# Dilated projections ahead of the gates among the filler products, and the last unit of the first mixer's output held back

## The chip, the cores and the metric

One core of a Trainium2 chip runs the whole program. The metric is the time of one execution in device microseconds (us), taken as the median of several runs. TensorE (PE) multiplies, ScalarE (ACT) and VectorE (DVE) read its results from PSUM, GpSimd (POOL) does small side work, SyncE (SP) issues the loads.

## What is computed

Two transformer blocks in sequence on 256 tokens of width 1024, in float32. The first has differential and stick-breaking attention, a cross attention and an MLP. The second, where the change lies, is cut here to what matters:

```python
proj = h @ w_in                       # queries, keys, values, gates of both mixers
q_a, k_c, v_c, k_s, v_s, k_w, v_w, g_nsa, q_b, k_b, v_b, g_ma, g_mb = split(proj)
y_a = nsa(rope(norm(q_a)), k_c, v_c, rope(norm(k_s)), v_s, rope(norm(k_w)), v_w, sigmoid(g_nsa))
y_b = dilated(rope(norm(q_b)), rope(norm(k_b)), v_b)      # 3 dilations, 4 heads each
m = sigmoid(g_ma) * (y_a @ w_o_a) + sigmoid(g_mb) * (y_b @ w_o_b)
x = x + m @ w_out                     # and the second block's MLP behind it
```

The first mixer (`nsa`) has 12 query heads in 3 key groups and adds three attentions: over keys compressed from blocks, over selected keys (`kts`) and over a window (`ktw`).

## The kernel before, in words

**Products.** Every float32 product is made of three fast ones: each operand is split into a high and a low part (`act` is `acth` and `actl`, a weight is `whi` and `wlo`), and PE runs high x high, low x high and high x low (L266 to L268 with the result transposed, L319 to L321 otherwise, L334 and L335 in the accumulation behind the mixers). A weight unit is 1024 x 256: SP loads it in two halves of 512 KB into `wraw` (6 buffers, L223), ACT copies the high part (L232), DVE subtracts for the low part (L233), 8 buffers each. One unit takes 48 such products (3 x 8 x 2), a unit of `w_o_a` 36.

**Order.** The program is written as attention steps with products put between them. A `Filler` holds a list of generators; `fill(n)` runs products from the first generator on until an amount `n` of work is done, and `flush()` runs all that is left. Out of this program a scheduler with its own estimates of durations makes the final order of each engine, and each engine then takes its instructions strictly in that order. Tiles share buffers by size class (`CLASSES`, L148): the biggest class, `c8` of 2048 floats a partition, has 8 buffers, used by the split activations, by the gates (`gm`), by the compression weights (`cw`) and by others.

**The second block.** `block2` projects the queries of the first group and all keys and values (`kv`, L1084). `nsa_keys` normalizes and rotates the keys: squares on ACT (L1151), their sums and an inverse root in small steps on DVE and ACT (L375 to L380), the scaling (L1156) and rotation (L1166, L1170) on DVE with POOL multiplying beside it (L1164); the result is `kn`, one tile for each 128 tokens. Its transposes on PE (L427) are evicted by ACT into `kts` and `ktw` (L619). The first `Filler` holds the query units 1 and 2 and the two compressions (L1036, with 1 MB loads of `cw`, L1032). Query evictions are L1178 (L1182 after the change, where `norm_rope_k`'s L1156, L1164, L1166, L1170 are L1160, L1168, L1170, L1174). The second `Filler` holds gate A (`gate_project`, 4 units), the dilated projections (`dil_project`, 9 units) and gate B, and, appended later, `first_mixer_out` (L1359), 4 units of the first mixer's output. They lie between the score and value steps of the first mixer and then of the two dilated head pairs (`dil_scores`, `dil_values`: transposes of probabilities L427, values L637 and L640, normalizer L1340). A pair's output is `dy` (L1428), split into `y`.

**The end of the mixers.** After the flush, the second mixer's output is accumulated over its two chunks of 128 (L266 to L268 into PSUM), weighted and added to the first mixer's (`evac_b`), split (L286 on ACT), and multiplied by `w_out` (L334). Matters for this end:

```python
acc = self.acc_new(True)
w = self.wrows(I["w_o_b_2"], 0)
for mp in range(4):
    for j in range(2):
        self.acc_add(acc, w, j, yc(6 + j), j == 0, j == 1, (2 * mp, 2 * mp + 1))
    evac_b(mp, acc[mp])
```

Of the kernel before, what the change touches and what calls it, by code (L numbers as in the profile page):

```python
# [10 lines left out]
F32R = mybir.dt.float32r  # L11
I32 = mybir.dt.int32
AF = mybir.ActivationFunctionType
# [4 lines left out]
P = 128  # L18
T = 256
NT = 2  # L20
D = 1024
KC = 8
HD = 64
# [102 lines left out]
def run(gen):  # L126
    for _ in gen:
        pass
# [6 lines left out]
class Builder:  # L135
# [381 lines left out]

    def sb_heads(self, q, k, v, ys, F):

# [3 lines left out]
        for c in range(2):  # L523
# [8 lines left out]
            for a in range(2):  # L532
                nc.scalar.activation(e[:, 2 * c + a], zs[2 * c + a][:, :384], AF.Abs)
        F.fill(3)
        x = nc.scalar.activation(e, e, AF.Exp, scale=-1.0)
        self.with_tables("natural_log", x, [lambda: nc.scalar.activation(e, e, AF.Ln, bias=self.one)])
        F.fill(3)
        ps, made = [], []
        for i, z in enumerate(zs):
            s = self.t([P, 384], "p", self.NP)  # L540
            nc.vector.scalar_tensor_tensor(out=s, in0=z[:, :384], scalar=0.0, in1=e[:, i], op0=ALU.max, op1=ALU.add)
            for c0 in (0, 256):
                self.strict(s[:, c0:c0 + P])
            F.fill(0.7)
            mm(z[:, 0:256], self.tri, s[:, 0:256], start=False, stop=True, skip_group_check=True)
# [7 lines left out]
            made.append(i)  # L553
        F.fill(1.5)
        for c in range(2):
# [3 lines left out]
            self.split1(ys[c][0], ys[c][1], po)  # L559
            F.fill(1)  # L560

# [524 lines left out]
    def nsa_keys(self, kv):  # L1086

        nc = self.nc
        gate = self.t([P, 3, NSA_H, 2], "gate")
        e = self.t([P, NT, 36], "gatee")  # L1090
        nc.scalar.activation(e, kv[:, :, 768:804], AF.Exp, scale=-1.0)
        nc.vector.tensor_scalar(out=e, in0=e, scalar1=1.0, scalar2=None, op0=ALU.add)
        for tt in range(NT):
            nc.vector.reciprocal(out=gate[:, :, :, 1 - tt], in_=e[:, tt].rearrange("p (h b) -> p b h", b=3))
        kn = [self.t([P, 6, 2, HD], "kn") for _ in range(NT)]
        xs = [kv[:, tt, 0:768].rearrange("p (a b) -> p a b", b=384)[:, :, 0:192].rearrange("p a (h d) -> p a h d", d=HD)
              for tt in range(NT)]
        self.norm_rope_k(xs, kn)
        kts = self.t([P, 3, 256], "kts")
        ktw = self.t([P, 3, 256], "ktw")  # L1100

        def transposed():
            for g in range(3):
                for dst, h in ((kts, g), (ktw, 3 + g)):
                    self.k_pair_t(dst[:, g, 0:256], [kn[tt][:, h] for tt in range(NT)])
            return kts, ktw, gate
        return transposed

    def cmp_keys(self, hk, hv):


        nc, mm = self.nc, self.nc.tensor.matmul
        o = self.Oo()
        for m in range(2):
            mm(o[0:48, 0:HD], hk[:, m], self.w2k[:, m], start=(m == 0), stop=(m == 1))
        kc = self.t([48, 1, HD], "kcn")
        nc.scalar.activation(kc[:, 0], o[0:48, 0:HD], AF.Copy)
        kcn = self.t([48, 1, 2, HD], "kcd")
        self.norm_rope([kc], lambda tt, i: self.rtc[:, i], [kcn[:, :, 0]], 1)
        nc.vector.tensor_copy(kcn[:, :, 1], kcn[:, :, 0])  # L1120
        ps = self.X()
        self.transpose(ps[:, 0:48], kcn.rearrange("p a b d -> p (a b d)"))
        kct = self.t([P, NSA_G, 2, 16], "kct")
        nc.gpsimd.memset(kct, 0.0)
        for a in range(2):
            rs = slice(64 * a, 64 * a + 64)
            nc.scalar.activation(kct[rs, :, a], ps[rs, 0:48].rearrange("p (g c) -> p g c", c=16), AF.Copy)
        rep = self.t([P, 2, 3, 4, 16], "hvrep")
        for m in range(2):
            nc.vector.tensor_copy(rep[:, m], hv[:, m].rearrange("p (g c) -> p g c", c=16)[:, :, None, :].to_broadcast(  # L1130
                [P, 3, 4, 16]))
        o = self.Oo()
        for g in range(3):
            for m in range(2):
                mm(o[0:64, g * HD:(g + 1) * HD], rep[:, m, g].rearrange("p r c -> p (r c)"), self.w2v[:, m],
                   start=(m == 0), stop=(m == 1))
        vx = self.t([P, 3, 4, HD], "vx")
        nc.gpsimd.memset(vx[64:128], 0.0)
        ov = o[0:64, 0:192].rearrange("p (g d) -> p g d", d=HD)
        for h in range(4):  # L1140
            nc.scalar.activation(vx[0:64, :, h], ov, AF.Copy, scale=self.headsel[:, h:h + 1])
        return kct, vx

    def norm_rope_k(self, xs, kn):

# [100 lines left out]
    def nsa_values(self, g, c, ps_, f, kv, vx, pct, y, F, work):  # L1246
        po = self.Oo((P, T))
        for b in range(2):
            for a in range(2):
                self.scale_rows(ps_[a, b], f[:, b, a])  # L1250
            pts = [self.probs_t(ps_[a, b]) for a in range(2)]
            if b == 0:
                self.nc.tensor.matmul(po, vx[:, g, 2 * c:2 * c + 2].rearrange("p a d -> p (a d)"), pct, start=True,
                                      stop=False, skip_group_check=True)
            F.fill(2 * work)
            vs = slice(192 + 384 * b + HD * g, 192 + 384 * b + HD * g + HD)
            self.pv2(po, [kv[:, 0, vs]] * 2, [kv[:, 1, vs]] * 2, pts, False, b == 1)
        self.split1(*y, po)
# [97 lines left out]
            nc.scalar.activation(s, s, AF.Ln, bias=self.one)  # L1356
            nc.scalar.activation(s, s, AF.Exp, scale=-1.0)

    def first_mixer_out(self, y, gates):  # L1359

        nc = self.nc
        for u in range(4):
            o = []
            w = self.wunit(self.I["w_o_a_2"][:, 256 * u:256 * u + 256].rearrange("(k p) n -> p k n", p=P), 6, 256)
            yield from self.gemm_t([w], y, o, nk=6)
            g = gates[0][:, 2 * u:2 * u + 2]
            nc.vector.tensor_tensor(out=g, in0=g, in1=o[0], op=ALU.mult)

    def block2(self, h):
        nc, I = self.nc, self.I  # L1370
        hc = lambda k: h[:, k]
        act = self.act(hc, self.gg)
        ss, ss2 = self.sumsq(h, self.g["g_final"])
        rf, rrn = self.rstd_n([ss, ss2], D, "rrn")
        rb = self.row(rrn, "rb")
# [7 lines left out]
        F = Filler(self.nsa_queries(act, rrn, 1, qs[1]), self.compress(bs[0], I["cmp_k_w1_2"], hk),  # L1383
                   self.nsa_queries(act, rrn, 2, qs[2]), self.compress(bs[1], I["cmp_v_w1_2"], hv))
        F.fill(FILL_KEYS)
        kts, ktw, gate = keys()
        F.fill(FILL_KEYS)
        self.nsa_queries_t(*qs[0])
        F.fill(1)
        y = (self.t([P, KC, T], "acth", dt=F32R), self.t([P, KC, T], "actl", dt=F32R))  # L1390
        yc = lambda k: (y[0][:, k], y[1][:, k])
        dil, gates = {}, []
        sc, pct = {}, {}
        sc[0, 0] = self.nsa_scores(0, 0, qs[0][0], kts, ktw, gate, F, FILL_SCORES)
        sc[0, 1] = self.nsa_scores(0, 1, qs[0][0], kts, ktw, gate, F, FILL_SCORES)
        F.flush()
        F = Filler(self.gate_project(act, rb, 4260, gates), self.dil_project(act, rrn, dil),
                   self.gate_project(act, rb, 5284, gates))
        kct, vx = self.cmp_keys(hk[0], hv[0])
        F.fill(2)  # L1400
        pc = self.nsa_cmp(0, qs[0][0], kct, gate)
        for g in range(NSA_G):
# [3 lines left out]
            pct = self.nsa_cmp_t(pc)  # L1406
            for c in range(2):
# [5 lines left out]
                elif c == 0:  # L1413
                    while 0 not in dil:
                        F.fill(1.0)
                    sc[0] = self.dil_scores(*dil[0][:2], F, FILL_DIL_SCORES)
        F.gens.append(self.first_mixer_out(y, gates))
        for pair in range(2):
            po = self.Oo((P, 2, T))
            values = self.dil_values(po, *sc.pop(pair), dil[pair][2], F, FILL_DIL_VALUES)  # L1420
# [10 lines left out]

        mx = (self.t([P, KC, T], "acth", dt=F32R), self.t([P, KC, T], "actl", dt=F32R))

        pins = []

        def evac_b(mp, o):
            sl = slice(2 * mp, 2 * mp + 2)
            g = gates[1][:, sl]
            a = nc.vector.tensor_tensor(out=g, in0=g, in1=o, op=ALU.mult)
            b = nc.vector.tensor_tensor(out=g, in0=g, in1=gates[0][:, sl], op=ALU.add)  # L1440
            pins.append((a, b, self.split1(mx[0][:, sl], mx[1][:, sl], g)))
        acc = self.acc_new(True)
        w = self.wrows(I["w_o_b_2"], 0)
        for mp in range(4):
            for j in range(2):
                self.acc_add(acc, w, j, yc(6 + j), j == 0, j == 1, (2 * mp, 2 * mp + 1))
            evac_b(mp, acc[mp])
        order = [pins[i][j] for i, j in ((0, 0), (0, 1), (1, 0), (1, 1), (0, 2), (2, 0), (2, 1), (1, 2),
                                             (3, 0), (3, 1), (2, 2), (3, 2))]
        for x, y in zip(order, order[1:]):  # L1450
# [3 lines left out]
        for k in range(KC):  # L1454
            i = nc.vector.scalar_tensor_tensor(out=h[:, k], in0=h[:, k], scalar=self.g["g_final"][:, k:k + 1],
                                               in1=rf, op0=ALU.mult, op1=ALU.mult)
# [62 lines left out]
```

## Time and profile before

| what | value |
|---|---|
| median of 3 runs | 881.71 us (881.45 to 884.4) |
| the profiled execution | 880.0 us, span 877.8 us |
| busy PE | 860.9 us (98%) |
| busy DVE, ACT, POOL | 602.1, 551.9, 95.6 us |
| granted clock of PE | 1.00 throughout |
| share of the last chain: PE, ACT, DMA, DVE | 92%, 3%, 2%, 2% |

Busy times are of one profiled execution, on the only core. PE is the engine that sets the time; the other engines' idle time costs nothing by itself. A matmul's own duration is drawn until its modelled end, so neighbours overlap: what counts is the distance between starts.

### The profile page before, as it was taken

To read this page: it belongs to the slowest core of one execution; us is meant where nothing else is said; L and a number is where in the kernel's file an instruction comes from. 1 tells how busy PE (TensorE), PEld (TensorE's weight loads), DVE (VectorE), ACT (ScalarE), POOL (GpSimd) and SP (SyncE) were. 2 spreads that over 40 slices of the span, in tenths; PEclk is the share of its full clock that TensorE was granted. 3 is DMA by queue.
4 is the path that set the end of the run, shared out by engine and by line. 5 is a ranking of instruction groups with operands and counts; after the bars stand their busy time and mean duration, and the time that the engine had idled before them with its cause. 6 is when DMAs were issued, how large, how long until landed. Compare 5 with 4: busy or idle time off the path is not lost.

```text
span 877.8 us, 18311 instructions
## 1 busy us (share of the span) xinstructions
PE 860.9 (98%) x7109; PEld 828.0 (94%) x7109; DVE 602.1 (69%) x1291; ACT 551.9 (63%) x1199; POOL 95.6 (11%) x139
## 2 busy tenths in 40 slices
PE   7999999999999999999999999999988999999998
PEld 6989999999999999999998999889978999999997
DVE  7645687585597555675877786686947975555554
ACT  5769577464575555664674887877764665555551
POOL 4032100020020000000203130113410300000000
PEclk9999999999999999999999999999999999999999
DMA  9655445653466766766387354232623565666541
GB/s 312 182 183 155 143 133 157 193 171 94 144 177 181 217 192 184 229 200 205 83 256 245 121 164 125 73 86 84 213 101 96 165 211 181 189 192 187 183 136 49
DMA packets 111830, 144.68 MB, mean 165 GB/s; under 512 B 6272, under 2 KB 100096, under 8 KB 111744
## 3 DMA queue, kind: packets, MB, share of 16 engines
q1 hardware_dynamic: 111600, 143.50, 53.2%
q8 instruction: 55, 0.90, 0.4%
q14 instruction: 31, 0.25, 0.1%
q10 hardware_dynamic: 144, 0.03, 0.0%
HBM read 142.46 MB, written 1.05 MB: 163 GB/s over the span
## 4 chain that ended last, share of the span: by engine, by line
PE 92%; ACT 3%; DMA 2%; DVE 2%; issue 1%; POOL 0%; SPq 0%; ACTq 0%; DVEq 0%; POOLq 0%
PE G L266 12%; PE G L267 12%; PE G L268 12%; PE G L320 5%; PE G L321 5%; PE G L319 5%; PE Z L268 4%; PE Z L267 4%; PE Z L266 4%; PE X L266 4%; PE X L268 4%; PE X L267 4%; PE X L427 3%; DMA wraw<-w_in 2%; PE Z L627 2%; PE O L640 1%
## 5 line engine op out<-in xcount | busy, mean ns | idle before, releaser
L233 DVE TENSOR_TENSOR wlo<-wraw,whi 128x512 fp32r<-128x512 f32 (+1 forms) x512 | 348.8, 696 | 167.4 <-ACT whi L232 164.6
L232 ACT ACTIVATE whi<-wraw 128x512 fp32r<-128x512 f32 (+1 forms) x512 | 313.6, 624 | 201.6 <-PE G L268 83.6
L267 PE MATMUL G<-acth,wlo 128*128 128x256 f32 x892 | 251.2, 283 | 4.3 <-DVE wlo L233 4.3
L266 PE MATMUL G<-acth,whi 128*128 128x256 f32 x892 | 252.3, 284 | 0.6 <-DVE gm L1352 0.3
L268 PE MATMUL G<-actl,whi 128*128 128x256 f32 x892 | 249.0, 283 | 0.0
L267 PEld LDWEIGHTS G<-acth,wlo 128*128 128x128 f32 x892 | 168.4, 189 | 6.0 <-DVE wlo L233 5.1
L266 PEld LDWEIGHTS G<-acth,whi 128*128 128x128 f32 x892 | 168.8, 189 | 2.6 <-issue 0.8
L268 PEld LDWEIGHTS G<-actl,whi 128*128 128x128 f32 x892 | 167.0, 189 | 0.3
L319 PE MATMUL G<-whi,acth 128*128 128x256 f32 x400 | 114.0, 286 | 0.0
L320 PE MATMUL G<-wlo,acth 128*128 128x256 f32 x400 | 114.0, 285 | 0.0
L321 PE MATMUL G<-whi,actl 128*128 128x256 f32 x400 | 114.0, 285 | 0.0
L320 PEld LDWEIGHTS G<-wlo,acth 128*128 128x128 f32 x400 | 75.5, 189 | 1.4 <-issue 0.8
L319 PEld LDWEIGHTS G<-whi,acth 128*128 128x128 f32 x400 | 75.4, 189 | 1.4 <-ACT whi L232 0.4
L321 PEld LDWEIGHTS G<-whi,actl 128*128 128x128 f32 x400 | 75.5, 189 | 1.0 <-issue 0.8
L266 PE MATMUL X<-mhl,whi 128*128 128x256 f32 x240 | 67.6, 282 | 0.5 <-DVE mt L1471 0.5
L268 PE MATMUL Z<-mhl,whi 128*128 128x256 f32 x240 | 67.5, 281 | 0.0
L268 PE MATMUL X<-mhl,whi 128*128 128x256 f32 x240 | 67.4, 281 | 0.0
L266 PE MATMUL Z<-mhl,whi 128*128 128x256 f32 x240 | 67.3, 281 | 0.0
L267 PE MATMUL X<-mhl,wlo 128*128 128x256 f32 x240 | 67.3, 280 | 0.0
L267 PE MATMUL Z<-mhl,wlo 128*128 128x256 f32 x240 | 67.3, 280 | 0.0
L266 PEld LDWEIGHTS X<-mhl,whi 128*128 128x128 f32 x240 | 45.3, 189 | 0.7 <-DVE mt L1471 0.7
L654 ACT ACTIVATE p<-p,mx 128x256 f32<-128x256 f32 x88 | 39.0, 446 | 10.2 <-DVE mx L647 6.1
(393 smaller groups left out, 1523.0 us busy)
## 6 DMA issues: line engine op xcount, KB each, us to landing
wraw<-w_up SPq DMA_DIRECT2D x64, 512.0 KB, 3.9
wraw<-w_down SPq DMA_DIRECT2D x64, 512.0 KB, 3.6
wraw<-w_in SPq DMA_DIRECT2D x42, 512.0 KB, 4.6
wraw<-w_dil SPq DMA_DIRECT2D x18, 512.0 KB, 4.1
wraw<-w_xkv SPq DMA_DIRECT2D x16, 512.0 KB, 3.7
wraw<-w_out SPq DMA_DIRECT2D x16, 512.0 KB, 3.7
wraw<-w_in SPq DMA_DIRECT2D x22, 256.0 KB, 5.5
wraw<-w_xq SPq DMA_DIRECT2D x8, 512.0 KB, 3.8
```

The source lines that it names most:

```text
L232: nc.scalar.activation(hi, r, AF.Copy)
L233: i = nc.vector.tensor_tensor(out=lo, in0=r, in1=hi, op=ALU.subtract)
L266: mm(out, w[0], x[0], start=first, stop=False, skip_group_check=True)
L267: mm(out, w[1], x[0], start=False, stop=False, skip_group_check=True)
L268: mm(out, w[0], x[1], start=False, stop=last, skip_group_check=True)
L319: mm(outs[tt], x[0][:, k, ts_], w[0], start=first, stop=False, skip_group_check=True)
L320: mm(outs[tt], x[0][:, k, ts_], w[1], start=False, stop=False, skip_group_check=True)
L321: mm(outs[tt], x[1][:, k, ts_], w[0], start=False, stop=(k == KC - 1), skip_group_check=True)
L427: self.mark = self.nc.tensor.transpose(out, in_, self.ident[:n, :n])
L627: i = mm(z[:, 0:256], q[rs, P:T], k[rs, 0:256], start=True, stop=True)
L640: mm(po[rs], v0[a], pts[a][:, 0:256], start=False, stop=last, skip_group_check=True)
L654: self.nc.scalar.activation(s[:, sl], s[:, sl], AF.Exp, scale=-1.0, bias=m[:, i:i + 1], accum_out=sums[:, i:i + 1])
```

## The change

Three edits. The dilated projections come first in the second `Filler`, then gate A and gate B. The transposed keys `kts`, `ktw` and the compressed values of groups 0 and 1 share one tile of the biggest class (`kt2`), the values of group 2 get a small one, and the tile pair `y` is taken only after the first flush. And `first_mixer_out` gets a list of units: 0 to 2 stay among the fillers, while unit 3 runs at the end, in the middle of the second mixer's accumulation, whose first chunk is now added for all outputs ahead of the second.

```diff
-        kts = self.t([P, 3, 256], "kts")
-        ktw = self.t([P, 3, 256], "ktw")
+        self.kt2 = self.t([P, 2048], "kt2")
+        kts, ktw = [self.kt2[:, 768 * i:768 * i + 768].rearrange("p (g k) -> p g k", k=256) for i in range(2)]
...
-        vx = self.t([P, 3, 4, HD], "vx")
-        nc.gpsimd.memset(vx[64:128], 0.0)
+        v01 = self.kt2[:, 1536:2048].rearrange("p (g h d) -> p g h d", g=2, d=HD)
+        v2 = self.t([P, 4, HD], "vx")
...
-    def first_mixer_out(self, y, gates):
+    def first_mixer_out(self, y, gates, us):
...
-        for u in range(4):
+        for u in us:
...
-        y = (self.t([P, KC, T], "acth", dt=F32R), self.t([P, KC, T], "actl", dt=F32R))
-        yc = lambda k: (y[0][:, k], y[1][:, k])
...
         F.flush()
-        F = Filler(self.gate_project(act, rb, 4260, gates), self.dil_project(act, rrn, dil),
+        y = (self.t([P, KC, T], "acth", dt=F32R), self.t([P, KC, T], "actl", dt=F32R))
+        yc = lambda k: (y[0][:, k], y[1][:, k])
+        F = Filler(self.dil_project(act, rrn, dil), self.gate_project(act, rb, 4260, gates),
                    self.gate_project(act, rb, 5284, gates))
...
-        F.gens.append(self.first_mixer_out(y, gates))
+        F.gens.append(self.first_mixer_out(y, gates, range(3)))
...
+        self.acc_add(acc, w, 0, yc(6), True, False)
         for mp in range(4):
-            for j in range(2):
-                self.acc_add(acc, w, j, yc(6 + j), j == 0, j == 1, (2 * mp, 2 * mp + 1))
+            self.acc_add(acc, w, 1, yc(7), False, True, (2 * mp, 2 * mp + 1))
             evac_b(mp, acc[mp])
+            if mp == 1:
+                run(self.first_mixer_out(y_a, gates, (3,)))
```

The scheduler makes a new order out of it. **PE, behind the second query unit.** `G_1088` (before) and `G_1087` (after) are that unit's result, `X` are banks for transposes, `kn` the keys, `Z` scores, `cw` compression weights; a "waits" names the engine whose result is awaited. Before:

```order
L321 MATMUL G_1088_6166<-whi_1086_6162,actl_970_5571 128x256
L1036 MATMUL G_1103_6268<-cw_1104_6269,bk_1017_5850 48x256 [waits DMAHW3_49]
L1036 MATMUL G_1103_6268<-cw_1104_6269,bk_1017_5850 48x256 x7
L1036 MATMUL G_1103_6268<-cw_1107_6287,bk_1017_5850 48x256 [waits DMAHW4_49]
L1036 MATMUL G_1103_6268<-cw_1107_6287,bk_1017_5850 48x256 x7
L319 MATMUL G_1139_6376<-whi_1131_6360,acth_969_5570 128x256 [waits Activation_49]
...
L319 MATMUL G_1139_6376<-whi_1137_6372,acth_969_5570 128x256
L427 MATMUL X_1089_6209<-c_ident_110,kn_1066_6107 128x128 [waits DVE_49]
L427 MATMUL X_1090_6213<-c_ident_110,kn_1066_6107 128x128
L320 MATMUL G_1139_6376<-wlo_1138_6373,acth_969_5570 128x256
```

After:

```order
L321 MATMUL G_1087_6165<-whi_1085_6161,actl_970_5571 128x256
L427 MATMUL X_1088_6208<-c_ident_110,kn_1066_6107 128x128 [waits DVE_49,Activation_49]
L427 MATMUL X_1089_6212<-c_ident_110,kn_1066_6107 128x128 [waits Activation_49]
L427 MATMUL X_1088_6208<-c_ident_110,kn_1067_6108 128x128 [waits DVE_49]
L427 MATMUL X_1089_6212<-c_ident_110,kn_1067_6108 128x128
L427 MATMUL X_1090_6216<-c_ident_110,kn_1066_6107 128x128 [waits Activation_49]
...
L427 MATMUL X_1105_6281<-c_ident_110,qn_1007_5771 128x128 [waits Activation_49]
L427 MATMUL X_1105_6281<-c_ident_110,qn_1007_5771 128x128
L627 MATMUL Z_1108_6290<-kt2_1075_6143,qt_1016_5849 128x256 [waits Activation_49]
...
L1036 MATMUL G_1102_6267<-cw_1103_6268,bk_1017_5850 48x256 [waits DMAHW4_49]
```

The key and query transposes and the first scores moved ahead of the compression product and of the whole third query unit (43 of its 48 products stood ahead of the first transposes before).

**ACT, around the keys' inverse root** (`rsy`; `qn` are the evicted queries of the second unit). Before:

```order
L232 ACTIVATE whi_1137_6372<-wraw_1130_6358 128x512 [waits DVE_49]
L376 ACTIVATE rsy_1072_6116<-rsv_1071_6115 128x12 [waits DVE_49]
L377 ACTIVATE rsy_1072_6116<-rsy_1072_6116 128x12 [waits Activation_49]
L232 ACTIVATE whi_1188_6590<-wraw_1186_6586 128x512 [waits DMAHW0_49,PE_49]
L232 ACTIVATE whi_1190_6594<-wraw_1186_6586 128x512 [waits PE_49]
L1178 ACTIVATE qn_1077_6145<-G_1088_6166,rrn_985_5640 128x256 [waits PE_49,Pool_49]
```

After:

```order
L232 ACTIVATE whi_1191_6602<-wraw_1186_6592 128x512 [waits DMAHW5_49,DVE_49,PE_49]
L376 ACTIVATE rsy_1072_6116<-rsv_1071_6115 128x12 [waits DVE_49]
L1182 ACTIVATE qn_1076_6144<-G_1087_6165,rrn_985_5640 128x256 [waits PE_49,Pool_49]
L377 ACTIVATE rsy_1072_6116<-rsy_1072_6116 128x12 [waits Activation_49]
L1182 ACTIVATE qn_1076_6144<-G_1087_6165,rrn_985_5640 128x256
```

The second step of the root now stands behind an eviction that waits for PE's second query unit.

**PE, at the end of the mixers.** `O_1672`, `G_1671` and their like are banks of the second mixer's accumulation, `Z_1687` and `Z_1686` the first of `w_out`. Before:

```order
L1340 MATMUL O_1615_8658<-diag_1617_8660,ones_68 64x256
L266 MATMUL O_1672_8970<-acth_1108_6290,whi_1677_8979 128x256 [waits DVE_49]
...
L268 MATMUL O_1672_8970<-actl_1109_6291,whi_1681_8987 128x256
L334 MATMUL Z_1687_9071<-acth_1667_8965,whi_1693_9079 128x256 [waits Activation_49]
```

After:

```order
L1344 MATMUL O_1592_8538<-diag_1594_8540,ones_68 64x256
L266 MATMUL O_1662_8920<-acth_1168_6534,whi_1667_8929 128x256 [waits DVE_49]
...
L268 MATMUL O_1662_8920<-actl_1169_6535,whi_1671_8937 128x256
L266 MATMUL G_1681_9001<-acth_1168_6534,whi_1675_8989 128x256 [waits DVE_49]
...
L268 MATMUL G_1681_9001<-actl_1169_6535,whi_1679_8997 128x256
L334 MATMUL Z_1686_9075<-acth_1657_8915,whi_1692_9083 128x256 [waits Activation_49]
```

The held unit's 36 products (`G_1681`) moved between the accumulation and the first product of `w_out`. On SP, the two pairs of `cw` loads, which stood between the two halves of the third query unit, now stand behind both and behind eight half units of `w_dil`.

## Rows read from the trace of the kernel before

**Rows 1.** The page: span and busy times of the engines.
```profile
span 877.8 us, 18311 instructions
PE 860.9 (98%) x7109; PEld 828.0 (94%) x7109; DVE 602.1 (69%) x1291; ACT 551.9 (63%) x1199; POOL 95.6 (11%) x139
```
**Rows 2.** Windows: length, busy PE, PEld, DVE, ACT, POOL (instructions), clock, DMA, GB/s.
```profile
460.00:470.00 10.00, 10.00 (x87) 8.27 (x86) 7.30 (x17) 5.96 (x14) 2.33 (x4) 1.00 1.10 347
470.00:480.00 10.00, 9.88 (x79) 7.37 (x78) 8.92 (x25) 3.10 (x9) 3.85 (x9) 1.00 0.59 183
...
650.00:660.00 10.00, 7.16 (x58) 4.98 (x54) 3.73 (x13) 7.12 (x23) 3.36 (x4) 1.00 0.34 107
660.00:670.00 10.00, 7.49 (x62) 6.68 (x62) 5.77 (x10) 4.12 (x8) 0.00 (x0) 1.00 0.00 0
```
**Rows 3.** Waits of PE, the longest sum: us, times, longest.
```profile
PE G L267 <- DVE wlo L233: 4.3, 4, 1.5
```
**Rows 4.** Timeline of PE, early stretch: start, us, operation, count [idle before <- releaser].
```profile
463.75 0.28 PE L320 MATMUL G<-wlo,acth 128*128 128x256 f32 x1
463.87 0.28 PE L321 MATMUL G<-whi,actl 128*128 128x256 f32 x1
464.08 3.66 PE L1036 MATMUL G<-cw,bk 128*48 128x256 f32 x32
...
473.13 0.44 PE L427 MATMUL X<-c_ident,kn 128*128 128x128 f32 x2
473.32 0.36 PE L320 MATMUL G<-wlo,acth 128*128 128x256 f32 x1
...
476.37 0.44 PE L427 MATMUL X<-c_ident,kn 128*128 128x128 f32 x2
```
**Rows 5.** Timeline of ACT, the same stretch.
```profile
463.25 1.15 ACT L232 ACTIVATE whi<-wraw 128x512 fp32r<-128x512 f32 x2 [3.26 <-DMA wraw<-w_in]
...
464.54 0.21 ACT L377 ACTIVATE rsy<-rsy 128x12 f32<-128x12 f32 x1
...
466.08 0.82 ACT L1178 ACTIVATE qn<-G,rrn 128x256 f32<-128x256 f32 x2
...
476.74 0.38 ACT L619 ACTIVATE kts<-X 128x256 f32<-128x256 f32 x1 [1.92 <-PE X L427]
477.02 0.38 ACT L619 ACTIVATE ktw<-X 128x256 f32<-128x256 f32 x1
```
**Rows 6.** Timeline of DVE, the same stretch.
```profile
465.32 0.17 DVE L379 TENSOR_TENSOR rsv<-rsv,rsy 128x12 f32<-128x12 f32 x1
...
466.98 1.02 DVE L1156 TENSOR_TENSOR nsq<-kv,nrs 128x384 f32<-128x384 f32 x2
...
473.00 0.34 DVE L1166 TENSOR_TENSOR nsq<-nsq,rt 128x192 f32<-128x192 f32 x1
...
474.15 1.01 DVE L1170 TENSOR_TENSOR kn<-nsq,nrb 128x384 f32<-128x384 f32 x2
```
**Rows 7.** Timeline of POOL, the same stretch.
```profile
467.67 4.31 POOL L1164 TENSOR_TENSOR nrb<-nsq,rt 128x96 f32<-128x96 f32 x8 [17.37 <-DVE nsq L1156]
```
**Rows 8.** Timeline of PE, end of the mixers: the five waits.
```profile
651.78 0.55 PE L427 MATMUL X<-c_ident,p 128*128 128x128 f32 x3 [0.69 <-ACT p L654]
654.17 0.55 PE L427 MATMUL X<-c_ident,p 128*128 128x128 f32 x3 [1.84 <-ACT pt L669]
...
660.33 0.44 PE L637 MATMUL O<-pt,dn 128*64 128x128 f32 x4 [0.64 <-ACT pt L669]
...
662.58 0.39 PE L266 MATMUL O<-acth,whi 128*128 128x256 f32 x1 [0.94 <-DVE dy L1428]
...
667.65 0.38 PE L334 MATMUL Z<-acth,whi 128*128 128x256 f32 x1 [1.24 <-ACT acth L286]
```
**Rows 9.** DMA issues, 440 to 470 us: KB each, median us from issue to landing.
```profile
cw<-cmp_k_w SPq DMA_DIRECT2D x2, 1024.0 KB, 7.5
cw<-cmp_v_w SPq DMA_DIRECT2D x2, 1024.0 KB, 10.3
```

More of the change, by code (lines that the diff above doesn't have):

```diff
@@ L1136, in cmp_keys @@
                    start=(m == 0), stop=(m == 1))
-        vx = self.t([P, 3, 4, HD], "vx")
-        nc.gpsimd.memset(vx[64:128], 0.0)
+        v01 = self.kt2[:, 1536:2048].rearrange("p (g h d) -> p g h d", g=2, d=HD)
+        v2 = self.t([P, 4, HD], "vx")
+        nc.gpsimd.memset(v01[64:128], 0.0)
+        nc.gpsimd.memset(v2[64:128], 0.0)
         ov = o[0:64, 0:192].rearrange("p (g d) -> p g d", d=HD)
         for h in range(4):
-            nc.scalar.activation(vx[0:64, :, h], ov, AF.Copy, scale=self.headsel[:, h:h + 1])
-        return kct, vx
+            nc.scalar.activation(v01[0:64, :, h], ov[:, 0:2], AF.Copy, scale=self.headsel[:, h:h + 1])
+            nc.scalar.activation(v2[0:64, h], ov[:, 2], AF.Copy, scale=self.headsel[:, h:h + 1])
+        return kct, [v01[:, 0], v01[:, 1], v2]
     def norm_rope_k(self, xs, kn):
@@ L1252, in nsa_values @@
             if b == 0:
-                self.nc.tensor.matmul(po, vx[:, g, 2 * c:2 * c + 2].rearrange("p a d -> p (a d)"), pct, start=True,
+                self.nc.tensor.matmul(po, vx[g][:, 2 * c:2 * c + 2].rearrange("p a d -> p (a d)"), pct, start=True,
                                       stop=False, skip_group_check=True)
@@ L1432, in block2 @@
         mx = (self.t([P, KC, T], "acth", dt=F32R), self.t([P, KC, T], "actl", dt=F32R))
-        pins = []
+        pins, y_a = [], y
         def evac_b(mp, o):
```

## The prediction

> **What bounds the kernel now.** I read the busy shares first, then busy time by window, then the timelines of the two places where the order of work changes. TensorE (PE) works 860.9 of 877.8 us [rows 1], so time is lost or won only where PE stands empty. In the two windows of 10 us from 460 to 480 it issues 87 and 79 matmuls and is busy 10.00 and 9.88 us; the two from 650 to 670 us hold 58 and 62, and are busy 7.16 and 7.49 [rows 2]. Outside those, the largest idle time is at the kernel's start, behind the first low halves of the weights (4.3 us in four waits, [rows 3]), which the change does not touch. So two places count. One is the **end of the dilated attention** in the second block, 650 to 668 us, where PE has run out of other products. The other is the **start of the compressed/selected attention**, 464 to 489 us, where PE is fully covered today [rows 2]: there the profile has a loss to give, not a gain.
>
> **The early stretch, term one.** In the kernel before, PE goes from the second query unit straight into the first compression product at 464.08, then into the third query unit; the first pair of key transposes comes at 473.13, right after the keys of the first token tile are ready, and the others lie among further products until 485 [rows 4]. Nothing is lost. In the changed order all twelve key transposes and four query transposes, and the first scores behind them, stand directly after the second query unit, ahead of the compression product and of the third query unit. PE takes its queue in order, so it waits for the whole chain of keys. I build that chain from durations before, in the order of the change.
>
> The second query unit's last matmul ends at 463.87 + 0.28 = 464.15 [rows 4]. ScalarE (ACT) now has a query eviction (L1182) ahead of the second step of the keys' inverse root (L377): 0.41, half of the pair's 0.82, then 0.21 [rows 5] gives 464.8. Three small VectorE (DVE) steps of some 0.17 [rows 6] give 465.3; no weight split stands among them any more. From the start of the scaled keys to the first GpSimd (POOL) operation is 466.98 to 467.67, 0.69, and POOL needs 4.31 for its eight [rows 6, 7]: 470.3. One rotation (0.34) and the second tile's two multiplications (1.01) [rows 6] give 471.6; seven handovers at an estimated 0.05 each, 472.0. Lower bound 471.6. Upper bound: the slower spacings that before shows, 2.23 from L377's end to the scaled keys (464.75 to 466.98) and 3.18 from POOL's end (471.98) to the keys' end (475.16), give 464.8 + 2.2 + 0.7 + 4.3 + 3.2 = 475.2.
>
> Then eight evictions pass through two banks of PSUM. One pair, from the transposes at 476.37 to the end of its second eviction at 477.40, takes 1.03 [rows 4, 5]: four in a row are 4.1, and ACT alone, at a spacing of 0.28, needs 2.6 with the first pair's 0.37 ahead. I take 3.6, nearer the full pair, because with two banks the next transposes can only start when an eviction ends. First scores at 475.6 (474.2 to 479.3). Of the time since 464.08 PE works only the sixteen transposes, at 0.19 for two [rows 4] 1.5 us. **Stall: 475.6 - 464.1 - 1.5 = 10.0 us (8.6 to 13.7).** No product lies behind those rows that could fill it, and nothing later pays it back, since the windows before 480 us are full already and the sum of the products is the same.
>
> **What stands behind the stall.** The 1 MB loads of the compression weights are issued after eight half units of the dilated weights now. The last of these needs a weight buffer that DVE frees just behind the scaled keys, about 466.5, so the first load goes out near 467.5; with the 7.5 us of [rows 9] it lands at 475.0, just ahead of its product. I take 0; if it takes the 10.3 us of the other pair it is late by 477.8 - 476.0 = 1.8. The load for the second half of the value compression waits for the first product to free its buffer, and holds SyncE's queue and its weight loads for that long; four dilated half-unit pairs are already in then, at 48 matmuls each some 22 us of PE's work: 0. The softmaxes of the first four score groups now come at PE one after the other without the gate products between: I take 0.9, half of the largest wait for a softmax that the trace has (1.84 [rows 8]); bounds 0 and 1.8.
>
> **The order of projections.** Dilated units ahead of the first gate change nothing by themselves in the middle: the products are the same, their number is, and the windows next to the early stretch [rows 2] are full. What they buy is that the dilated tiles exist early, so that the last pair's scores can stand well before the end. One shared tile for keys and values, and the later start of `y`, only move buffers: no operation but one memset and four copies, on POOL and ACT, off the chain: 0.
>
> **The tail, term two.** Before, PE waits 0.69 and 1.84 for probabilities, 0.64 for the last transposed ones, 0.94 for the dilated output `dy`, and 1.24 for the first split of the mixer's sum [rows 8]. In the changed order, units 0 to 2 of the first mixer's output lie between the last value steps, so the three waits for probabilities go. The held unit's 36 matmuls, 36 x 0.117 = 4.2 us, lie between the last product of the second mixer and the one that waits for the split, so the 1.24 goes. The wait for `dy` stays: nothing but accumulations that need it stand behind. Gone are 0.69 + 1.84 + 0.64 + 1.24 = 4.4; each wait also hides that a matmul drawn as 0.28 makes room for the next after 0.12 (463.75 to 463.87, [rows 4]), 4 x 0.16 = 0.6 more. **Gain 5.0**; at least 3.2 if the split is still late when the held unit ends, at most 5.9 if `dy` is covered too.
>
> **Sum.** +10.0 - 5.0 + 0.9 = +5.9 us on a profiled execution of 880.0 (span 877.8): 885.9. The runs' median, 881.7, lies 1.7 above that execution, so I forecast **887.6**. Its own ends are 8.6 - 5.9 = +2.7 (884.4) and, all that is bad together, 13.7 - 3.2 + 1.8 + 1.8 = +14.1; half-way up from the forecast is 892.
>
> **Rivals.** *The clock falls (0.28).* PE is empty from 464.1 to about 470.9, and only sparsely busy until 475.6. The two windows with 2.84 and 2.51 us of PE idle time still have granted clock 1.00 [rows 2], but the longest single wait in them is 1.84 [rows 8], so these rows do not settle it. If PE comes back at the lower of its two levels, the work directly behind, like the 32 records of compression product that take 3.66 [rows 4], runs twice as long: 3.7 more, 891.3. The Trainium skill, TensorE: Matmul & The Clock Gate, section HAM oscillation, says that a wait which leaves the engine idle long enough brings the slow clock back; no row of this trace shows it, and by that rule the rival would be the forecast.
>
> *The keys come early, faster (0.08).* Before, ACT waited 3.26 for a weight transfer ahead of the keys' inverse root (the whi copy at 463.25 [rows 5]); if the chain no longer hung on the end of the second query unit, it could start 3 us sooner and pass beside that unit's matmuls. It wins if first scores come before 469.7 (a stall of 4.1, with the 0.9 just what the tail returns). With a stall of 1 the time is 881.7 - 5.0 + 1 = 877.7. Against it: the eviction that stands ahead waits for the last matmul of that unit, and POOL's 4.31 comes after.
>
> *It all but cancels (0.15).* Chain at its lower bound, `dy` covered, softmaxes covered: +2.7, 884.4, inside what can be told from no change.
>
> **Chances.** A measurement of this kernel can tell about 0.5%, 4.4 us, from no change: 877.3 to 886.1 is "same". The forecast has 0.49, of which I put 0.12 below 886.1; with the cancelling case, same is 0.27, slower 0.37 + 0.28 = 0.65, faster 0.08. The range, 882.0 to 892.5, takes in the cancelling case, the forecast to its upper half and the clock; the fast rival (0.08) and the upper tails, some 0.1, stay out.
>
> **What would show it.** Right: a PE hole near 464 to 471 in the changed profile, its first transposes waiting for VectorE's keys, then for ACT's evictions; first scores near 475.6; later products shifted by 10; at the end no wait for probabilities, only one near 0.9 for `dy`. Wrong: no window under 8 busy us of 10 between 460 and 480; or waits for probabilities of over 1 us still there at the end. A granted clock under 1.00 after the hole decides for the first rival.

## The result and the profile after

The changed kernel takes **889.3 us** (median of 4, 887.07 to 889.55) against 881.58 us before (median of 4): ratio 1.0074, 95% interval 1.0055 to 1.0094. It is slower, by 7.7 us between the medians where 5.9 were forecast (the ratio, which is not that of the two medians, stands for 6.5 us, its interval for 4.8 to 8.3); the forecast of 887.6 lies 1.7 below, and the range of 882.0 to 892.5 holds it. From the profile's page of one execution of 889.55 us: span, busy times, and the granted clock of PE in 40 equal slices, in tenths of full speed ([rows 1] before):

```profile
span 887.8 us, 18317 instructions
...
PE 866.5 (98%) x7109; PEld 830.9 (94%) x7109; DVE 602.7 (68%) x1291; ACT 555.5 (63%) x1203; POOL 94.2 (11%) x140
...
PEclk9999999999999999999997999999999999999999
```

PE has the same 7109 matmuls, and yet 5.6 us more of busy time: some of them ran slower. Below are windows of the two places, and of a third that the prediction did not have ([rows 2] before; length, busy PE, PEld, DVE, ACT, POOL, clock, DMA, GB/s):

```profile
460.00:470.00 10.00, 4.37 (x37) 4.17 (x36) 8.64 (x21) 5.29 (x15) 3.60 (x8) 0.98 0.87 274
470.00:480.00 10.00, 7.69 (x32) 4.42 (x34) 6.54 (x22) 3.81 (x12) 2.15 (x5) 0.51 1.04 339
...
580.00:585.00 5.00, 3.33 (x30) 2.27 (x30) 5.00 (x16) 3.71 (x12) 1.30 (x2) 1.00 0.37 105
585.00:590.00 5.00, 4.88 (x28) 4.26 (x28) 4.12 (x19) 4.17 (x14) 1.91 (x2) 0.66 0.36 93
650.00:660.00 10.00, 10.00 (x89) 8.95 (x89) 6.06 (x12) 8.31 (x21) 3.61 (x5) 1.00 0.61 195
660.00:670.00 10.00, 9.06 (x79) 7.25 (x78) 4.26 (x8) 4.28 (x9) 0.00 (x0) 1.00 0.52 170
```

From 460 to 480 PE issues 69 matmuls instead of 166, and the clock there is the lower of its two levels; the end of the mixers, 650 to 670, is full but for one gap. The early stretch on PE's timeline ([rows 4] before):

```profile
464.09 0.28 PE L321 MATMUL G<-whi,actl 128*128 128x256 f32 x1
471.26 0.66 PE L427 MATMUL X<-c_ident,kn 128*128 128x128 f32 x2 [6.89 <-DVE rsv L378]
472.58 0.69 PE L427 MATMUL X<-c_ident,kn 128*128 128x128 f32 x2 [0.66 <-DVE kn L1174]
473.52 2.27 PE L427 MATMUL X<-c_ident,kn 128*128 128x128 f32 x8 [0.26 <-ACT kt L619]
475.85 1.12 PE L427 MATMUL X<-c_ident,qn 128*128 128x128 f32 x4
477.00 1.23 PE L627 MATMUL Z<-kt,qt 64*128 64x256 f32 x4
...
478.58 2.49 PE L1036 MATMUL G<-cw,bk 128*48 128x256 f32 x16
481.00 0.38 PE L319 MATMUL G<-whi,acth 128*128 128x256 f32 x1
```

And the chain that PE waited for, on ACT, DVE and POOL ([rows 5 to 7] before):

```profile
464.47 0.47 ACT L1182 ACTIVATE qn<-G,rrn 128x256 f32<-128x256 f32 x1 [0.75 <-PE G L321]
464.84 0.20 ACT L377 ACTIVATE rsy<-rsy 128x12 f32<-128x12 f32 x1
...
465.69 1.03 DVE L1160 TENSOR_TENSOR nsq<-kv,nrs 128x384 f32<-128x384 f32 x2
...
471.49 1.03 DVE L1174 TENSOR_TENSOR kn<-nsq,nrb 128x384 f32<-128x384 f32 x2
...
466.40 3.83 POOL L1168 TENSOR_TENSOR nrb<-nsq,rt 128x96 f32<-128x96 f32 x8 [15.88 <-DVE nsq L1160]
```

The chain is the one forecast, step by step: ACT's root behind the eviction at 464.84 (forecast start 464.6), scaled keys at 465.69 (465.3), POOL done at 470.23 (470.3), last keys at 472.52 (472.0), first scores at 477.00 (475.6). The waits of PE at the new third place and at the end ([rows 8] before):

```profile
584.87 0.41 PE L427 MATMUL X<-c_ident,dn 128*128 128x128 f32 x2 [1.67 <-DVE mx L1213]
585.40 1.11 PE L627 MATMUL Z<-kt,qt 64*128 64x256 f32 x4
...
587.25 0.41 PE L267 MATMUL G<-acth,wlo 128*128 128x256 f32 x1
...
669.63 0.39 PE L266 MATMUL O<-acth,whi 128*128 128x256 f32 x1 [0.94 <-DVE dy L1432]
```

Near 583 PE waits for a rotated dilated tile (`dn`; the releaser named is a small DVE step that ended just then, the tile itself was finished right before it), and the matmuls behind are drawn at 0.41 instead of 0.28: the clock is low for 3.4 us, from 585.6 on. At the end only the wait for `dy` is left; 0.69, 1.84, 0.64 and 1.24 are gone. So is a wait that the kernel before had in its middle, for an evicted dilated tile:

```profile
577.54 0.55 PE L427 MATMUL X<-c_ident,p 128*128 128x128 f32 x3 [0.56 <-ACT dxt L612]
```

**The account, profile against profile (+10.0 us of span).** From 464.2 to 481.0 pass 16.8 us. The work in it, at full speed, is 1.5 for sixteen transposes, 0.9 for the first scores (483.89 to 484.74 for the next ones) and 1.9 for half a compression product: 4.2, so 12.6 are lost. The hole near 583 costs 1.7 and the low clock behind it 1.7, less the 0.7 that the wait at 577.5 cost before (0.56, and 0.16 as reckoned in the prediction). The end gains 5.0. Sum +10.3. The medians differ by less, 7.7, since the profiled execution of before is one of its best: it ran at clock 1.00 all through, as 11 of 70 further executions of that kernel did, while the other 59 have a mean clock of 0.989 to 0.998 and, but for three, take 881.4 or more.

### The profile page after: what moved, and what is told of

Its sections match the earlier page's. It is cut to its first block, busy times and chain, and to the rows that moved or that the text cites. A ratio compares the mean times of both kernels' runs of the same rounds, so it can differ in the third digit from the quotient of the medians.

```text
span 887.8 us, 18317 instructions
## 1 busy us (share of the span) xinstructions
PE 866.5 (98%) x7109; PEld 830.9 (94%) x7109; DVE 602.7 (68%) x1291; ACT 555.5 (63%) x1203; POOL 94.2 (11%) x140
## 4 chain that ended last, share of the span: by engine, by line
PE 94%; DVE 3%; DMA 1%; issue 0%; ACT 0%; POOL 0%; SPq 0%; DVEq 0%; POOLq 0%; ACTq 0%
PE G L266 12%; PE G L267 12%; PE G L268 12%; PE G L320 6%; PE G L321 6%; PE G L319 6%; PE Z L268 4%; PE Z L267 4%; PE Z L266 4%; PE X L266 4%; PE X L268 4%; PE X L267 4%; PE X L427 3%; PE Z L627 2%; DMA wraw<-w_in 1%; PE O L640 1%
## 5 line engine op out<-in xcount | busy, mean ns | idle before, releaser
L267 PEld LDWEIGHTS X<-mhl,wlo 128*128 128x128 f32 x240 | 45.4, 189 | 0.0
```

The source lines that it names most:

```text
L267: mm(out, w[1], x[0], start=False, stop=False, skip_group_check=True)
```

## The experiments

**Which edit makes the early stall.** The prediction took the order of the three edits together. The first version has the tiles alone, that is the shared key tile and the later `y`; against the change:

```diff
-        F = Filler(self.dil_project(act, rrn, dil), self.gate_project(act, rb, 4260, gates),
+        F = Filler(self.gate_project(act, rb, 4260, gates), self.dil_project(act, rrn, dil),
...
-        F.gens.append(self.first_mixer_out(y, gates, range(3)))
+        F.gens.append(self.first_mixer_out(y, gates, range(4)))
...
-        self.acc_add(acc, w, 0, yc(6), True, False)
...
```

(and the accumulation as in the kernel before)

> Only the shared key tile and the later y of the change; gate A first and no held unit, as before the change. Theory: the shared tile takes a buffer of the biggest class ahead of the compression weights, so these load late and the scheduler puts the key transposes first; the whole early stall with its lower clock is here (PE empty near 464 to 471, granted clock 0.5 for some 9 us), while the end of the mixers waits as before: 881.6 + 12 = 893 to 894 us. Rival, the dilated projections in front make the early order: no early stall, 881 to 882 us.

Measured: 888.92 us, ratio 1.0076 (1.0055 to 1.0097). Windows of this version:

```profile
460.00:470.00 10.00, 4.29 (x37) 4.09 (x35) 8.72 (x21) 5.45 (x16) 3.69 (x8) 0.82 0.89 268
470.00:480.00 10.00, 7.76 (x32) 4.47 (x34) 6.46 (x22) 3.88 (x13) 2.07 (x5) 0.50 1.04 338
580.00:590.00 10.00, 10.00 (x85) 9.65 (x85) 8.78 (x28) 8.80 (x31) 3.23 (x4) 1.00 0.47 132
```

The whole early stall is there with gate A in front, and no hole near 583: its cause is the edit of the tiles, not the order of the projections. SyncE's loads of the compression weights show what it did. The first two lines are of the kernel before, the last two of this version:

```profile
445.01 1.12 SPq L1032 DMA_DIRECT2D cw<-cmp_k_w  x2
446.24 6.18 SPq L1032 DMA_DIRECT2D cw<-cmp_v_w  x2
...
467.88 1.12 SPq L1032 DMA_DIRECT2D cw<-cmp_k_w  x2
469.11 12.52 SPq L1032 DMA_DIRECT2D cw<-cmp_v_w  x2
```

The loads go out 23 us later, as in the change (467.96). No run has the shared tile without the later `y`; the version with 18 units below tells the two apart in part.

The time came out 4 to 5 lower than expected. The end did not wait as before: only 0.64, 0.94 and 1.24 are left, the waits of 0.69 and 1.84 are gone although nothing at the end was edited, which makes some 2.9 with the 0.16 for each. The wait of 0.56 near 577 is gone too, 0.7. Profile against profile that leaves 12.6 - 2.9 - 0.7 = 9.0, and 8.8 were measured (886.6 - 877.8); the rest is that the profiled execution of before is one of its best.

**The held unit alone on the kernel before.**

```diff
-        F.gens.append(self.first_mixer_out(y, gates))
+        F.gens.append(self.first_mixer_out(y, gates, range(3)))
...
+            if mp == 1:
+                run(self.first_mixer_out(y_a, gates, (3,)))
```

> Only the held unit and the new order of the second mixer's accumulation on the kernel before. Theory: early stretch covered as before; the wait of 1.24 for the split goes, but the unit is missing among the fillers, so the waits for probabilities at the end grow by up to its 4.2 us: 881.6 - 1.4 to 881.6 + 2.8, likeliest 881. Rival, the held unit alone makes the tail's gain of 5: 876.6.

Measured: 883.49 us, ratio 1.0011 (0.9999 to 1.0023). PE waits 2.4 for probabilities where it waited 1.84, and a wait of 1.2 for the pair's split comes in place of the 1.24 for the mixer's; the clock is 0.66 over 650 to 660. So it gains nothing by itself; the theory's range of 880.2 to 884.4 held, its likeliest of 881 did not: the unit is missing among the fillers.

**The shared tile taken after the compression weights.** One number is the filler work written ahead of the key transposes, which are the first to fill the shared tile. By the theory it decides whether the weights of the compression get their buffers of the biggest class before that tile or after it:

```diff
-        F.fill(FILL_KEYS)
+        F.fill(18)
         kts, ktw, gate = keys()
```

> The change with one number altered: 18 instead of 4 units of filler work before the keys' transposes are written, so that the compression weights take their buffers ahead of the shared key tile. Theory: PE has the compression product and the third query unit ahead of the key transposes again, no hole at 464, clock 1.00 there; the hole near 583 and its low clock stay: 889.3 - 12 = 877 us. Rival, the early stall is only moved to the next wait for keys or weights: 885 us or more.

Measured: 883.67 us, ratio 1.0024 (1.0009 to 1.0038). The hole at 464 is gone (PE busy 10.00 and clock 1.00 from 460 to 480), but the gain of 5.6 is half of what was expected: PE waits 1.5 and 0.7 near 532 and 1.6 and 0.7 near 546, for softmaxes and a rotated tile, and the clock is low after each. The profiled execution is the slowest of the twelve (886.85). Its windows from 530 to 538, and two from 436 to 440 that the last section uses:

```profile
436.00:438.00 2.00, 2.00 (x15) 2.00 (x15) 1.39 (x5) 0.41 (x2) 0.00 (x0) 0.76 0.48 82
438.00:440.00 2.00, 2.00 (x12) 2.00 (x11) 0.76 (x5) 0.00 (x0) 0.00 (x0) 0.50 1.02 348
...
530.00:534.00 4.00, 1.79 (x14) 1.39 (x15) 3.39 (x18) 2.02 (x8) 0.00 (x0) 0.83 0.60 176
534.00:538.00 4.00, 4.00 (x19) 3.06 (x18) 1.69 (x10) 2.49 (x11) 0.00 (x0) 0.50 0.01 2
```

Its loads of the compression weights go out at 447.12 and 448.34, three of the four, and the last at 481.26. The later `y` is still in this version, so `y` alone does not hold the loads back; and three instead of four early loads fit one buffer less. That the shared tile works through its buffer is read from these times and the order, and not tested by itself.

**The clock by itself.** Matmuls of ones by ones, into the bank of the first key transposes, keep PE busy while it waits (their results are overwritten); one filler step more is written ahead of the keys.

```diff
+        for _ in range(warm):
+            i = self.nc.tensor.matmul(ps[:, 0:P], self.ones, self.ones, start=True, stop=True)
+            self.after(i, self.last_n)
```

> The change with sixteen matmuls of ones by ones added on PE in front of the first key transpose, behind the second query unit (and one filler step more before the keys), so that PE is busy for some 6.5 us of its hole; nothing waits less for data. Theory: the stall stays 10 us, but the clock stays at 1.00 through the transposes, scores and compression product: 2.4 us less, 886.9 us. Rival, the clock costs nothing of its own because the keys and evictions set the pace: 889.3 us. Other rival: the sparse transposes behind the added work bring the clock down all the same, 889 us with clock 0.5 later.

> The version with added matmuls of ones, 33 instead of 16, so that PE is busy through its whole hole (7.7 us, up to about 471.7); data arrive as late as before. Theory: the empty hole is what brings the clock down, so it stays at 1.00 through transposes, scores and compression product; first scores at 475.9 instead of 476.8: 1 to 1.5 us under the 886.2 of the version with 16, 885 us. Rival, the sparse transposes and evictions behind bring it down all the same: 886 us or more, granted clock 0.5 somewhere between 472 and 482.

With 16: 886.2 us, ratio 1.0048 (1.0031 to 1.0065). The added matmuls ran nearly twice as fast as reckoned, 3.73 us in all, so PE still stood empty from 467.8 to 471.0 and the clock was low from 469.9 to 476.7. With 33: 887.79 us, ratio 1.0066 (1.0049 to 1.0084), yet what it was made for is plain. Neither total is the price of the clock: in both versions the hole near 583 is gone as well (PE busy 5.00 of 5.00 us from 580 to 585 and clock 1.00). What tells is the early stretch of the version with 33. Its timeline and windows (in this version line 427 is 429, 627 is 632, 1036 is 1041):

```profile
465.78 7.53 PE L620 MATMUL X<-ones 128*128 128x128 f32 x66
473.14 0.38 PE L429 MATMUL X<-c_ident,kn 128*128 128x128 f32 x2
...
477.69 0.70 PE L632 MATMUL Z<-kt,qt 64*128 64x256 f32 x4 [0.20 <-ACT qt L614]
...
480.41 0.39 PE L320 MATMUL G<-whi,acth 128*128 128x256 f32 x1
```

```profile
470.00:475.00 5.00, 4.01 (x35) 3.54 (x33) 4.70 (x13) 0.90 (x4) 2.03 (x6) 1.00 0.95 290
475.00:480.00 5.00, 4.41 (x34) 2.79 (x36) 3.19 (x12) 3.05 (x11) 1.70 (x4) 1.00 1.10 348
```

With PE busy through the wait the clock stays at 1.00, through the sparse transposes too, and from the second query unit's end to the third one's start pass 480.41 - 465.78 = 14.6 us, not 16.8. The clock was worth 2.2 us in this stretch; the remaining 10.4 are the wait for keys and evictions. The total of the version with 33 missed its 885: new waits of 0.9, 0.9 and 0.6 stand near 550, of an order that the scheduler made anew, and in the profiled execution the clock is low from 437 to 440.3; whether that is all of it was not traced.

**Gate A in front again, held unit kept.** The edit is the first one of the first experiment's diff.

> The change with gate A ahead of the dilated projections again (shared key tile and held unit stay). Theory: the early stall stays; the hole near 583 with its low clock goes (3.4 us), but with the held unit gone from the fillers and the last pair's scores late, waits for probabilities of 2 to 4 us come back at the end, as in the version with the held unit alone: 889.3 - 3.4 + 3 = 889, between 887 and 891. Rival, the dilated projections in front are what the tail lives on: 891 or more. Other rival, they buy nothing: 886.

Measured: 888.82 us, ratio 1.0072 (1.0051 to 1.0093), as the theory had it: no hole near 583, clock 1.00 there, and waits of 1.18, 0.64 and 0.94 at the end (1.18 and 0.64 for probabilities, 0.94 for `dy`). What the dilated projections in front gain at the end, they give back near 583.

**Without the held unit.**

```diff
-        F.gens.append(self.first_mixer_out(y, gates, range(3)))
+        F.gens.append(self.first_mixer_out(y, gates, range(4)))
```

(and the accumulation as before)

> The change without the held unit (all four units among the fillers, accumulation as before). Theory: the wait of 1.24 for the first split comes back and no wait for probabilities: 889.3 + 1.4 = 890.7 us. Rival, the unit is worth as much among the fillers as held: 889.3 us.

Measured: 890.44 us, ratio 1.0099 (1.0077 to 1.0121). PE waits 1.3 for the split again and for nothing else at the end; the wait of 0.94 for `dy`, which the change has, is gone. So by its waits the unit is worth some 0.3 to 0.4, by the medians 1.1, and the intervals of the two ratios overlap: that holding it helps is not shown by the total.

**The second hole.**

```diff
-TRANSPOSE_DELAY = 2
+TRANSPOSE_DELAY = 3
```

> The change with the transposes of the dilated keys and queries put one projection unit later (delay 3 instead of 2). Theory: the hole of 1.7 near 583, where PE waits for a rotated dilated tile, and the 3.4 us at half clock behind it go: 889.3 - 3.4 = 885.9 us. Rival, VectorE is the bound in that stretch and the wait only moves: 889 us.

Measured: 885.25 us, ratio 1.0041 (1.0026 to 1.0056), 4 us less than the change. A wait of 0.97 for a transposed probability stays near 582, the clock there is 1.00, and the wait for `dy` is gone as well. DVE is as full there as in the change (5.00 of 5.00 from 580 to 585), so the rival did not hold: it is the place of the transposes that made the hole.

**Both stalls taken away.** 12 units of filler work ahead of the key transposes, and the delay of 3.

> The change with 12 instead of 4 units of filler work before the key transposes, and the delay of 3: both stalls taken away. Theory: only an eviction-paced stretch of some 2 us stays at 475, no deep hole, clock at or near 1.00: 889.3 - 12 + 2 - 3.4 = 876 us, under 879. Rival, as with 18 units, softmaxes and dilated tiles without cover open new holes between 530 and 555: 882 us or more.

Measured: **878.82 us, ratio 0.9964 (0.9950 to 0.9978)**: faster than the kernel before by 0.36%. The largest waits of its PE (us in all, times, longest):

```profile
PE G L267 <- DVE wlo L233: 3.3, 3, 1.4
PE X L427 <- ACT kt L619: 1.3, 3, 0.9
PE Z L438 <- DVE ones L434: 1.1, 1, 1.1
PE O L637 <- ACT pt L669: 1.0, 1, 1.0
```

Of the early stall only evictions are left (1.3 for the keys, 0.5 for the queries), of the end nothing. It was 2.8 above the 876 forecast: the clock fell in most of its executions (0.991 to 0.998), in the profiled one at the kernel's start and from 478.7 to 485.6; the three at 1.00 took 877.3 to 877.9. Its loads of the compression keys go out at 446.68, early as before.

**Three more versions around it.**

> 12 units of filler work before the key transposes with gate A in front of the dilated projections (shared tile and held unit as in the change, delay 2). Theory: the early stall goes as with the dilated projections in front, 888.8 - 10 = 879 us, and waits for probabilities of some 2 us stay at the end; then putting the dilated projections first is worth at most 1 us against 878.8. Rival, without the dilated projections in front the end costs 4 to 5: 883 us.

Measured: 884.84 us, ratio 1.0034 (1.0021 to 1.0046). The rival held: with the early stall gone, having the gate in front costs 0.94, 1.52 and 0.94 at the end. (A wait of 1.5 for the compressed keys is there too, but also in the last version below, which has the dilated projections in front.) Together with the later transposes, the dilated projections in front are worth 6 us by the medians; the three waits are 3.4 of it, the rest was not traced.

> 14 instead of 12 units of filler work before the key transposes, delay 3: the whole third query unit and the compression product ahead of the transposes, products among the last evictions. Theory: no wait for keys, evictions partly covered, 1 to 2 us less than the 878.8 of the version with 12: 877.5 us. Rival, holes between 530 and 555 as with 18 units: 881 or more.

Measured: 883.33 us, ratio 1.0019 (1.0007 to 1.0031): a miss. The key transposes together wait for evictions (1.9) and the compression's transposes ahead of them for DVE (1.3), and two waits for softmaxes, 0.6 and 1.0, stand near 569 and 580; the clock is 0.83 from 470 to 480 and 0.66 behind.

> The best version so far (12 units, delay 3) without the held unit. Theory: the wait of 1.24 for the first split comes back, as it did in the change without the held unit (+1.1): 878.8 + 1.2 = 880 us. Rival, with this order the unit is needed among the fillers for a wait near the end (1.0 there now): 878.8 or less.

Measured: 879.15 us, ratio 0.9956 (0.9940 to 0.9972). No wait for the split came back, PE goes from the second mixer's accumulation at 666.89 to the first product of `w_out` at 667.01; that the held unit is worth anything in this order is not to be seen.

## Why the prediction was right, point by point

- **The early stretch, term one: right in place, cause in the queue, and size.** Forecast stall 10.0 (8.6 to 13.7), at full clock 10.4 by the version with added matmuls. Handovers and evictions were a little slower than reckoned (first scores 477.00, of which about 1 us is the low clock). What the prediction had wrong is the edit that makes it: it took the shared tile and the later `y` at 0, as something that only moves buffers, and these two alone, with no other edit, make the whole stall (888.92).
- **Behind the stall.** The compression weights went out at 467.96 (forecast 467.5), landed after 8.0 us and were in time: 0 as taken. The term of 0.9 for softmaxes without cover was wrong, there is no such wait between 477 and 580: 0.
- **The order of projections, taken as 0: the step that failed.** "The products are the same" is true of the work, not of the waits. Projections in front bring their normalized tiles, their rotation and their transposes into the stretch where DVE is already full (5.00 of 5.00 us busy from 580 to 585), and PE met a transpose before its tile: 1.7, and 1.7 for the clock behind. The hole is there in the two profiles with these projections in front and the delay and filler work of the change (the change and the one without the held unit), and not in those with gate A in front. Putting these transposes one unit later took away 4 us, the wait for `dy` among them.
- **The tail, term two: right.** Forecast gain 5.0, and the profile shows just the four named waits gone and `dy` left at 0.94. Their causes were less simple. The waits of 0.69 and 1.84 went with the tiles alone, so that they went because units 0 to 2 lie between the value steps is not shown; the 0.64 is there in the two versions with the gate in front and the change's filler work, and gone with the dilated projections in front, with the held unit or without. The held unit takes away the 1.24, but without it the 0.94 for `dy` goes in its place.
- **The clock, the first rival: it came true.** Chance 0.28 and price 3.7; it fell, and cost 2.2 early and 1.7 near 583. It should have had more than half. The Trainium skill (TensorE: Matmul & The Clock Gate, section HAM oscillation) says that a wait which leaves the engine idle long enough brings the slow clock back. This trace agrees behind the early hole: clock 0.50 in the work right behind an empty PE, 1.00 there when PE was kept busy. The length of a hole alone does not tell, though: behind the 1.67 near 583 the clock fell, behind the 1.84 at the end of the mixers in the kernel before it stayed at 1.00.
- **The keys come early: did not happen.** The root stood behind the eviction, as was said against it.
- **The sum.** +5.9 forecast, +7.7 measured. Profile against profile it is 10.4 + 2.2 + 3.4 - 0.7 - 5.0 = +10.3, 4.4 more than forecast; adding the 1.7 by which before's median stands above its profiled execution was wrong for a kernel whose profiled execution lies at its own median. The two errors were of opposite sign, so that the forecast came within 1.7 is in part luck. The stall came out by the mechanism that was forecast, the tail in its four waits; the clock and the hole near 583 were outside the sum.

## What to carry to other kernels

An edit of buffers is an edit of the order: here a tile that takes a buffer of a scarce class came before a load's tile, the load went out 23 us later, and a scheduler with its own estimates put other work first, whose real inputs were not ready. So look, in the new order, for the first instruction behind each full stretch of the bound engine that waits for a long chain on other engines, and build that chain from measured rows. A hole in TensorE's work cost its own length and, in two places here, the work behind it at half speed (2.2 us behind the hole of 6.9, 1.7 behind that of 1.7); and work moved forward needs its side chains (normalizing, rotating, evicting) priced where they land.

## What the runs showed that was not expected

- The clock also fell where PE had no wait at all. In the profiled executions of three versions, those with 18 units, with 33 added matmuls and with 12 units without the held unit, it is 0.50 from about 437 to 440.3 with PE busy 2.00 of 2.00 us (the first two rows of the version with 18 units above); in others, the kernel before among them, it is 1.00 there. In the 2 us ahead PE runs sums with a single output column (L388), in the kernel before as well. 3.4 us at half clock are 1.7 us; the kernel before takes 880.2 at mean clock 1.00 and 881.6 at 0.998 (medians of 11 and 23 executions), 1.4 apart, so such a stretch may be what many of its executions have. Why it falls there in some executions stays open; no run here was made for it.
- Sixteen added matmuls of ones took 3.73 us, 0.12 for each of 32 records, where the twenty records of the same kind at the start of the kernel before take 4.05, 0.20 each, with a granted clock of 1.00 in both rows. What slows the first ones was not tried.
